# The last expert's down projection by column halves, each half scaled and scattered on its own

## The chip, the cores and the metric

The kernel runs on one core of one Trainium2 chip. The metric is device microseconds (us) of one execution, the median of several runs. Times inside a run are given from the start of the profiled span.

## The reference

One layer of a diffusion backbone: a token mixer (a bidirectional linear recurrence and an attention branch), then an expert-choice mixture of 16 experts over 1024 tokens of 1024 channels. The change lies in the mixture, cut here to its core:

```
aff = softmax(h @ w_router)                      # 1024 tokens x 16 experts
gate, idx = top_k(aff.T, 128)                    # each expert takes 128 tokens
xg  = h[idx]                                     # 128 x 1024 per expert
hid = silu(xg @ w_e_gate[e]) * (xg @ w_e_up[e])  # 128 x 1024
y   = (hid @ w_e_down[e]) * gate                 # 128 x 1024, scaled row by row
out = x + mod5 * zeros.at[idx].add(y)            # rows scattered, added to the output
```

## The kernel before

Weights and activations are fp32. Each matrix product is made of three matmuls (`mm3`, lines 98 to 100): both operands are split into a high part (`eh`, written by ScalarE as a cast, line 94) and a low rest (`el`, written by VectorE as a difference, line 95), and high x high, high x low and low x high are summed in PSUM. An expert's weight matrix comes as four loads of 1 MB (`load_raw`, line 990, issued by SyncE (SP), raw tiles `me` and `ma` in a ring of fifteen), each with two blocks of 128 rows and all 1024 columns. A split pair (`eh`, `el`) serves twelve matmuls. There are three buffers for `eh` and two for `el`, so the `el` of a pair can be written only when TensorE (PE) has read the `el` of two pairs before.

For each expert e, `up(e)`, `gate(e + 1)` and `down(e)` follow each other on PE, whose order is that of the code. `split_hid` turns the hidden 128 x 1024 tile by eight transposes (`hdt`) and splits it (`hdh` by ScalarE, `hdl` by VectorE (DVE)). `down(e)` runs 48 matmuls of 512 columns into a PSUM tile `w_e_down` of 128 x 1024, block of rows after block of rows, both column halves of each. Then DVE scales the whole tile once (`y`, line 1311, by the gate column `gcol` and the row `bc5`), and GpSimd (POOL) issues an indirect DMA (line 1312) that adds the 128 rows of `y`, 4 KB each, to the rows of the output named by `icol`. For all experts but the last, `split_hid(e)` is run in the middle of `gate(e + 1)`; for the last it stands ahead of `down`, with nothing between.

All scatters add into the same output, and each waits on POOL until the one before it has landed. The names DMASW and DMAHW below are the counters of landed DMAs that POOL and SP issued, and DVE_49, PE_49 and Activation_49 count the instructions that those engines have finished; an instruction that waits for a count waits for all earlier instructions of that engine too. DVE takes its instructions strictly in the order shown.

Of the kernel before, what the change touches and what calls it, by code (L numbers as in the profile page):

```python
# [19 lines left out]
F32 = mybir.dt.float32  # L20
F32R = mybir.dt.float32r
I32 = mybir.dt.int32
U32 = mybir.dt.uint32
AF = mybir.ActivationFunctionType
OP = mybir.AluOpType
AX = mybir.AxisListType

P = 128
D = 1024
KD = D // P  # L30
# [18 lines left out]
NE = 16  # L49
# [11 lines left out]
def layer_kernel(ctx: ExitStack, tc: tile.TileContext, I, rope_tab, out, dbg=None):  # L61
    nc = tc.nc
# [6 lines left out]
    x, w_in, w_ada = I["x"][0], I["w_in"][0], I["w_ada"][0]  # L69
# [17 lines left out]
    def pa(name="pa"):  # L87
        return ps["p"].tile([P, 1024], F32, name=name, tag="a", bufs=3)
# [4 lines left out]
    def split(h, l, src):  # L93
        nc.scalar.copy(h, src)  # L94
        nc.vector.tensor_tensor(l, src, h.bitcast(F32), OP.subtract)  # L95

    def mm3(o, lh, ll, rh, rl, start, stop):
        nc.tensor.matmul(o, lh, rh, start=start, stop=False)  # L98
        nc.tensor.matmul(o, lh, rl, start=False, stop=False)  # L99
        nc.tensor.matmul(o, ll, rh, start=False, stop=stop)  # L100
# [10 lines left out]
    def krows(w, c0, n):  # L111
        return w[:, c0:c0 + n].rearrange("(k p) n -> p k n", p=P)
# [142 lines left out]
    for m in range(2):  # L255
        for k in range(KD):
            if m == 0 or k < 4:
                nc.tensor.transpose(modv[:, m * KD + k, :], mrow[m][:, k * P:(k + 1) * P], ident[0:2, 0:2])
            else:
                for w in range(2):  # L260
# [5 lines left out]
                                   op0=OP.add, op1=OP.mult)  # L266
# [33 lines left out]
    n = n_early  # L300
# [30 lines left out]
    def nextw(shape, look=None):  # L331
        n = taken[0]
        assert items[n][1] == shape, (items[n], shape)
        taken[0] = n + (LOOK if look is None else look)
        fetch()
        taken[0] = n + 1
        return ahead[n]
# [31 lines left out]
    for j in range(NFIRST):  # L369
        h, l = nextw([KD, P])  # L370
# [48 lines left out]
    with pool("p2") as p2:  # L419
        wqh = p2.tile([P, KD, Z2], F32R, name="wqh")  # L420
        wql = p2.tile([P, KD, Z2], F32R, name="wql")
        for j in range(4):
            raw = wst.tile([P, 2, Z2], F32, name="wr", tag="wr", bufs=4)
# [3 lines left out]
        for j in range(2):  # L427
            raw = wst.tile([P, HEADS * QD], F32, name="wr", tag="wr", bufs=4)
# [3 lines left out]
        raw = wst.tile([P, 2, 512], F32, name="wr", tag="wr", bufs=4)  # L432
# [164 lines left out]
    if True:  # L597
# [106 lines left out]
        with tc.manual_schedule(engines={mybir.EngineType.Activation, mybir.EngineType.PE}):  # L704
# [4 lines left out]
            nlam, mag, z, s, s2, p_, p8, m8 = (sp[:, j] for j in range(8))  # L709
# [49 lines left out]
    for e in range(2):  # L759
        for nm, val in (("h", 1.0), ("l", 0.0)):  # L760
# [4 lines left out]
                                    op0=OP.mult, op1=OP.add)  # L765
# [92 lines left out]
    for b in range(KD):  # L858
        if b < 2:
            po, h, l = early[b]  # L860
            ro_mm(po, h, l, [KD - 1])
        else:
            h, l = nextw([KD, P])
            po = pa("ro")
# [30 lines left out]
    with pool("p5a") as p5a:  # L895
# [44 lines left out]
        with tc.manual_schedule(engines={mybir.EngineType.PE}):  # L940
            nxt = scores(0, 0)
            for i, (h, kt) in enumerate(steps):
                ph, pl = nxt
                if kt == 0:
                    po = [ps["p"].tile([P, 512], F32, name="po", bufs=2) for _ in range(2)]
# [13 lines left out]
                for n in range(2):  # L959
                    side(2 + n)  # L960
                    sl = slice(n * 512, (n + 1) * 512)
# [20 lines left out]
    xring, xsplit, raws, used = [], [], [], [0]  # L982

    def load_raw():

        n = len(raws)
        nm, e, k = worder[2 * n]
        pl, tg, nb = xring[n % (NME + NMA) >= NME]
        raw = pl.tile([P, 2, D], F32, name=tg, tag=tg, bufs=nb)
        nc.sync.dma_start(raw, krows(I[nm][0, e, k * P:(k + 2) * P, :], 0, D))  # L990
        raws.append(raw)

    pairs = []

    def split_raw():
        n = len(pairs)
        while len(raws) <= n:
            load_raw()
        h = xsplit[0].tile([P, 2, D], F32R, name="eh", bufs=3)
        l = xsplit[0].tile([P, 2, D], F32R, name="el", bufs=2)  # L1000
        split(h, l, raws[n])
        pairs.append((h, l))
# [6 lines left out]
    with pool("p6b", side="right") as p6b, pool("p6", side="right") as p6:  # L1009
# [119 lines left out]
        with tc.manual_schedule(engines={mybir.EngineType.PE}):  # L1129
            for hf in range(2):  # L1130
# [15 lines left out]
                else:  # L1146
# [17 lines left out]
                    while len(raws) < NME - 2:  # L1164
                        load_raw()
                for ph in (2 * hf, 2 * hf + 1):
                    if ph == 2:
                        for j in range(4):
                            wo[2, j] = wo[1, j]
                    for t in range(4):  # L1170
                        if t == 3 and ph in (0, 2):
                            load_wo(ph + 1, 0)
                        if t == 0 and ph in (1, 3):
                            for j in range(1, 4):
                                load_wo(ph, j)
                            if ph == 3:
                                while len(raws) < NME:
                                    load_raw()
                        if ph == 3 and t in (1, 2):
                            split_raw()  # L1180
                        xo(ph, t)
# [9 lines left out]
    gcol = consts.tile([P, NE], F32, name="gcol")  # L1191
    icol = consts.tile([P, NE], I32, name="icol")
    with pool("p7a", side="right") as p7a, pool("p7", side="right") as p7:
        xring.append((p7a, "ma", NMA))
        bc5 = p7.tile([P, D], F32, name="bc5")
        nc.sync.dma_start(bc5, bcast(mod_d[3], D))
        VT = ("hdh", "hdl", "y", "silu")
        def pq(name):
            return ps["p"].tile([P, 1024], F32, name=name, tag="q", bufs=4)
# [51 lines left out]
        XR, XG, G, H, HT = {}, {}, {}, {}, {}  # L1251
        out_rows = out[0]
# [9 lines left out]
        def tsplit(src, nm):  # L1262
            nb = 2 if nm == "xg" else 1
            hh = p7.tile([P, KD, P], F32R, name=nm + "h", tag=nm + "h", bufs=nb)
            ll = p7.tile([P, KD, P], F32R, name=nm + "l", tag=nm + "l", bufs=nb)
            tp = pq(nm + "t")
            for k in range(KD):
                nc.tensor.transpose(tp[:, k * P:(k + 1) * P], src[:, k * P:(k + 1) * P], ident)
            split(hh, ll, tp.rearrange("p (k t) -> p k t", t=P))
            return hh, ll  # L1270
# [6 lines left out]
        def proj(nm, e, op_, mid=None, km=4):  # L1277
            po = pq(nm)
            for k in range(KD):
                if k == km and mid:  # L1280
                    mid()
                h, l = wk(nm, e, k)
                for n in range(2):
                    sl = slice(n * 512, (n + 1) * 512)
                    mm3(po[:, sl], op_[0][:, k], op_[1][:, k], h[:, sl], l[:, sl], k == 0, k == KD - 1)
            return po
# [4 lines left out]
        def split_hid(e):  # L1291
            HT[e] = tsplit(H.pop(e), "hd")
# [7 lines left out]
        def up(e):  # L1300
# [2 lines left out]
            nc.vector.tensor_tensor(hid, po, hid, OP.mult)  # L1303
            H[e] = hid

        def down(e):
            if e + 1 == NE:
                split_hid(e)
            po = proj("w_e_down", e, HT.pop(e))
            y = p7.tile([P, D], F32, name="y", tag="y", bufs=1)  # L1310
            nc.vector.scalar_tensor_tensor(y, po, gcol[:, e:e + 1], bc5, op0=OP.mult, op1=OP.mult)  # L1311
            nc.gpsimd.indirect_dma_start(out=out_rows, out_offset=bass.IndirectOffsetOnAxis(ap=icol[:, e:e + 1], axis=0),  # L1312
                                         in_=y, in_offset=None, compute_op=OP.add)
# [7 lines left out]
        for e in range(NE):  # L1321
            up(e)
            if e + 2 < NE:
                gather(e + 2)
            if e + 1 < NE:
                gate(e + 1)
            down(e)
# [40 lines left out]
```

## Time and profile before

| | |
|---|---|
| median of 3 runs | 1769.93 us (1767.58 to 1776.2) |
| profiled execution, its own time | 1771.81 us |
| its span, first to last instruction | 1769.8 us |
| PE busy | 1687.1 us, 95% of the span |
| DVE busy | 1313.4 us, 74% |
| ACT (ScalarE) busy | 1014.9 us, 57% |
| POOL busy | 264.5 us, 15% |
| mean granted clock of TensorE | 0.981 of full speed |

PE is busy nearly all the time, but the busy share is a mean over the span. The change touches only what follows the last expert's hidden tile, some 22 us, and what counts there is which engine waits for which. The profiled execution is 1.88 us longer than the median.

### The profile page before, as it was taken

Reading aid. Unit: us, or ns where it says so; the run is one execution under the profiler, and the core shown is the slowest. Engines: PE = TensorE matmul, PEld = TensorE weight load, DVE = VectorE, ACT = ScalarE, POOL = GpSimd, SP = SyncE. Lnnn points to the kernel's source line nnn. Section 1 sums busy time; section 2 is a strip of 40 time slices with the busy share of each in tenths; the row PEclk is TensorE's granted clock in tenths of the full one; section 3 lists DMA queues with packets and bytes.
Section 4 is the critical chain, followed back from the end, with each engine's and each line's share of the span. In section 5 each row is a group of like instructions: output and inputs, shape, how many; then the busy total and the mean of one; then the engine's idle time right before and its main releaser. Section 6 shows DMA issues by size and latency. Waiting matters only on the chain.

```text
span 1769.8 us, 20838 instructions
## 1 busy us (share of the span) xinstructions
PE 1687.1 (95%) x7823; PEld 1356.9 (77%) x7823; DVE 1313.4 (74%) x1607; ACT 1014.9 (57%) x1105; POOL 264.5 (15%) x196
## 2 busy tenths in 40 slices
PE   8999999999999999999999999939999999999996
PEld 3788887888887877777777678827888888888885
DVE  4755456788886454787877657587999999989996
ACT  2533324876788313667776532316777777777773
POOL 1123331211221100111210100020121111112101
PEclk9999999999999999999999999969999999999999
DMA  8264444435443934000000355667999999999981
GB/s 328 100 181 101 108 121 140 131 126 167 155 144 117 318 136 152 28 28 28 29 1 1 138 199 213 234 261 286 379 395 391 403 399 381 399 402 380 389 309 24
DMA packets 174179, 363.72 MB, mean 206 GB/s; under 512 B 40160, under 2 KB 90744, under 8 KB 174080
## 3 DMA queue, kind: packets, MB, share of 16 engines
q1 hardware_dynamic: 168896, 343.54, 53.6%
q0 software_dynamic: 5184, 18.88, 4.0%
q8 instruction: 61, 1.00, 0.2%
q14 instruction: 38, 0.31, 0.0%
HBM read 314.84 MB, written 47.54 MB: 205 GB/s over the span
## 4 chain that ended last, share of the span: by engine, by line
PE 71%; DVE 11%; ACT 6%; issue 4%; DMA 4%; POOL 3%; SPq 0%; POOLq 0%; DVEq 0%; ACTq 0%
PE w_e_gate L99 3%; PE w_e_gate L100 3%; PE w_e_gate L98 3%; PE w_e_down L99 3%; PE w_e_down L100 3%; PE w_e_down L98 3%; PE w_e_up L99 3%; PE w_e_up L98 3%; PE w_e_up L100 3%; PE z L99 2%; PE z L98 2%; PE z L100 2%; PE pm L816 2%; POOL st L143 2%; PE s L98 2%
## 5 line engine op out<-in xcount | busy, mean ns | idle before, releaser
L95 DVE TENSOR_TENSOR el<-ma,eh 128x2048 fp32r<-128x2048 f32 x114 | 258.2, 2286 | 22.2 <-PE w_e_down L99 10.8
L94 ACT CAST eh<-ma 128x2048 fp32r<-128x2048 f32 x114 | 217.9, 1917 | 73.7 <-PE w_e_up L100 28.7
L95 DVE TENSOR_TENSOR el<-me,eh 128x2048 fp32r<-128x2048 f32 x78 | 176.9, 2287 | 16.6 <-ACT eh L94 6.0
L94 ACT CAST eh<-me 128x2048 fp32r<-128x2048 f32 x78 | 149.0, 1916 | 47.4 <-PE w_e_gate L100 17.3
L906 ACT ACTIVATE pr<-s 128x512 f32<-128x512 f32 x160 | 95.8, 599 | 77.2 <-PE s L100 75.8
L818 DVE TENSOR_REDUCE mx<-pm 128x1 f32<-128x320 f32 x256 | 114.4, 483 | 22.8 <-PE pm L816 20.6
L99 PE MATMUL z<-xl,wh 128*128 128x512 f32 x320 | 125.2, 392 | 1.9 <-DVE xl L280 1.9
L98 PE MATMUL z<-xh,wh 128*128 128x512 f32 x320 | 125.2, 393 | 1.0 <-DVE xh L279 0.8
L100 PE MATMUL z<-xh,wl 128*128 128x512 f32 x320 | 125.0, 391 | 1.2 <-POOL wl L326 1.2
L1312 POOL DMA_INDIRECT out_dram<-y,icol x16 | 52.3, 3268 | 469.9 <-DVE y L1311 469.9
L94 ACT CAST wh<-wr 128x1024 fp32r<-128x1024 f32 (+1 forms) x53 | 52.0, 980 | 116.1 <-PE z L99 55.0
L95 DVE TENSOR_TENSOR pl<-pr,ph 128x1024 fp32r<-128x1024 f32 x64 | 81.0, 1265 | 31.4 <-ACT ph L94 24.7
L99 PE MATMUL w_e_up<-el,xgh 128*128 128x512 f32 x256 | 100.7, 394 | 0.6 <-DVE el L95 0.6
L98 PE MATMUL w_e_gate<-eh,xgh 128*128 128x512 f32 x256 | 101.1, 395 | 0.2 <-ACT xgh L94 0.2
L99 PE MATMUL w_e_gate<-el,xgh 128*128 128x512 f32 x256 | 101.2, 395 | 0.0
L100 PE MATMUL w_e_gate<-eh,xgl 128*128 128x512 f32 x256 | 100.1, 391 | 0.8 <-DVE xgl L95 0.8
L98 PE MATMUL w_e_down<-eh,hdh 128*128 128x512 f32 x256 | 99.7, 389 | 1.1 <-ACT hdh L94 1.1
L98 PE MATMUL w_e_up<-eh,xgh 128*128 128x512 f32 x256 | 100.7, 393 | 0.0
L99 PE MATMUL w_e_down<-el,hdh 128*128 128x512 f32 x256 | 100.6, 393 | 0.0
L100 PE MATMUL w_e_down<-eh,hdl 128*128 128x512 f32 x256 | 99.9, 390 | 0.5 <-DVE hdl L95 0.5
L100 PE MATMUL w_e_up<-eh,xgl 128*128 128x512 f32 x256 | 99.8, 390 | 0.0
L816 PE MATMUL pm<-kh,qh 97*128 97x320 f32 x256 | 86.6, 353 | 7.0 <-DVE kl L95 4.1
(349 smaller groups left out, 4368.7 us busy)
## 6 DMA issues: line engine op xcount, KB each, us to landing
ma<-in_w_e_down_dram SPq DMA_DIRECT2D x40, 1024.0 KB, 9.4
ma<-in_w_e_up_dram SPq DMA_DIRECT2D x38, 1024.0 KB, 8.0
ma<-in_w_e_gate_dram SPq DMA_DIRECT2D x36, 1024.0 KB, 7.2
me<-in_w_e_gate_dram SPq DMA_DIRECT2D x28, 1024.0 KB, 7.0
me<-in_w_e_up_dram SPq DMA_DIRECT2D x26, 1024.0 KB, 8.2
me<-in_w_e_down_dram SPq DMA_DIRECT2D x24, 1024.0 KB, 9.8
wr<-in_w_in_dram SPq DMA_DIRECT2D x32, 512.0 KB, 4.5
wr<-in_w_ada_dram SPq DMA_DIRECT2D x32, 512.0 KB, 4.2
```

What stands on the lines that cost most here:

```text
L94: nc.scalar.copy(h, src)
L95: nc.vector.tensor_tensor(l, src, h.bitcast(F32), OP.subtract)
L98: nc.tensor.matmul(o, lh, rh, start=start, stop=False)
L99: nc.tensor.matmul(o, lh, rl, start=False, stop=False)
L100: nc.tensor.matmul(o, ll, rh, start=False, stop=stop)
L143: nc.gpsimd.tensor_tensor(ap, ap, h, OP.pow)
L816: nc.tensor.matmul(pm[:, 0:320], qh[:, t * P:(t + 1) * P], kh[:, g * 320:(g + 1) * 320], start=True, stop=True)
L818: nc.vector.tensor_reduce(mx[:, g, t:t + 1], pm[:, 0:320], axis=AX.X, op=OP.max)
L906: nc.scalar.activation(pr[:, sl], sp_, AF.Exp)
L1312: nc.gpsimd.indirect_dma_start(out=out_rows, out_offset=bass.IndirectOffsetOnAxis(ap=icol[:, e:e + 1], axis=0), in_=y, in_offset=None, com ...
```

## The change

The four loads of the last expert's `w_e_down` are cut differently: each now holds four blocks of 128 rows and 512 columns, in the order rows 0 to 511 and rows 512 to 1023 of the left columns, then the same of the right columns. `last_down` runs all 24 matmuls of the left half, then scales that half (128 x 512) and scatters it as rows of 512 columns into the output seen as 2048 rows of 512; then the same for the right half. The row numbers are 2 x `icol` and 2 x `icol` + 1, made by two DVE instructions of 128 x 1 (`ic2`). The first half's `y` has the buffer of `y`, the second's that of `silu`. Both halves of the product lie in one PSUM tile, as before.

```diff
+        if (nm, e) == ("w_e_down", NE - 1):
+
+            raw4, n4 = raw.rearrange("p a (b n) -> p (a b) n", b=2), k // 2
+            nc.sync.dma_start(raw4, krows(I[nm][0, e, n4 % 2 * 512:(n4 % 2 + 1) * 512, :], n4 // 2 * 512, 512))
+        else:
+            nc.sync.dma_start(raw, krows(I[nm][0, e, k * P:(k + 2) * P, :], 0, D))
...
+        def last_down(e):
+
+            split_hid(e)
+            hh, hl = HT.pop(e)
+            halves = out_rows.rearrange("s (a n) -> (s a) n", a=2)
+            ic2 = p7.tile([P, 2], I32, name="ic2")
+            for n in range(2):
+                nc.vector.tensor_scalar(ic2[:, n:n + 1], icol[:, e:e + 1], 2.0, float(n), op0=OP.mult, op1=OP.add)
+            po = pq("w_e_down")
+            for n in range(2):
+                sl = slice(n * 512, (n + 1) * 512)
+                for k in range(KD):
+                    m = used[0] // 2
+                    while len(pairs) <= m + k // 4:
+                        split_raw()
+                    h, l = (x.rearrange("p a (b n) -> p (a b) n", b=2)[:, k % 4] for x in pairs[m + k // 4])
+                    mm3(po[:, sl], hh[:, k], hl[:, k], h, l, k == 0, k == KD - 1)
+                used[0] += 4
+                y = p7.tile([P, 512], F32, name="y", tag=("y", "silu")[n], bufs=1)
+                nc.vector.scalar_tensor_tensor(y, po[:, sl], gcol[:, e:e + 1], bc5[:, sl], op0=OP.mult, op1=OP.mult)
+                nc.gpsimd.indirect_dma_start(out=halves, out_offset=bass.IndirectOffsetOnAxis(ap=ic2[:, n:n + 1], axis=0),
+                                             in_=y, in_offset=None, compute_op=OP.add)
+
         def down(e):
             if e + 1 == NE:
-                split_hid(e)
+                return last_down(e)
```

Three places show what moves. First PE, in the last `down`: the 23rd to the 26th of its 48 matmuls, and the 37th and 38th, which are the first of the fourth pair. Before:

```order
7158 L99 MATMUL w_e_down<-el,hdh 128x512
7159 L100 MATMUL w_e_down<-eh,hdl 128x512
7160 L98 MATMUL w_e_down<-eh,hdh 128x512
7161 L99 MATMUL w_e_down<-el,hdh 128x512 [waits DVE_49]
...
7172 L98 MATMUL w_e_down<-eh,hdh 128x512 [waits Activation_49]
7173 L99 MATMUL w_e_down<-el,hdh 128x512 [waits DVE_49]
```

Now, the same places:

```order
7158 L99 MATMUL w_e_down<-el,hdh 128x512
7159 L100 MATMUL w_e_down<-eh,hdl 128x512
7160 L98 MATMUL w_e_down<-eh,hdh 128x512 [waits DVE_49]
7161 L99 MATMUL w_e_down<-el,hdh 128x512
...
7172 L98 MATMUL w_e_down<-eh,hdh 128x512 [waits Activation_49]
7173 L99 MATMUL w_e_down<-el,hdh 128x512
```

The wait for DVE has moved from the 26th matmul, the first that reads the third pair's `el`, to the 25th, the first of the right half; and the 38th, the first that reads the fourth pair's `el`, no longer waits for DVE.

Second DVE, at the end of the program: the `el` of the last two pairs and what follows. Before:

```order
1361 L95 TENSOR_TENSOR hdl<-hdt,hdh 128x1024 [waits Activation_49]
1362 L95 TENSOR_TENSOR el<-ma,eh 128x2048 [waits DMAHW2_49,DVE_49,PE_49]
1363 L95 TENSOR_TENSOR el<-ma,eh 128x2048 [waits DVE_49,DMAHW3_49,PE_49,Activation_49]
1364 L1311 SCALAR_TENSOR_TENSOR y<-w_e_down,gcol,bc_9508 128x1024 [waits DMASW2_49,PE_49]
1365 L1364 UNCONDITIONAL_BRANCH
```

Now, the same instructions of DVE:

```order
1363 L95 TENSOR_TENSOR hdl<-hdt,hdh 128x1024 [waits Activation_49]
1364 L95 TENSOR_TENSOR el<-ma,eh 128x2048 [waits DMAHW2_49,DVE_49,PE_49]
1365 L95 TENSOR_TENSOR el<-ma,eh 128x2048 [waits DVE_49,DMAHW3_49,PE_49,Activation_49]
1366 L1330 SCALAR_TENSOR_TENSOR y<-w_e_down,gcol,bc_9508 128x512 [waits DMASW2_49,PE_49]
1367 L1330 SCALAR_TENSOR_TENSOR y<-w_e_down,gcol,bc_9508 128x512 [waits PE_49]
1368 L1392 UNCONDITIONAL_BRANCH
```

The first half's `y` stands behind the `el` of the fourth pair, which belongs to the right half.

Third POOL, its last DMAs (the scatters of the 14th and the 15th expert, and what the 16th has). Before:

```order
164 L1312 DMA out_dram<-y,icol 1024x1024 [waits DMASW7_49,DVE_49]
165 L1312 DMA out_dram<-y,icol 1024x1024 [waits DMASW1_49,DVE_49]
166 L1312 DMA out_dram<-y,icol 1024x1024 [waits DMASW2_49,DVE_49]
167 L1364 UNCONDITIONAL_BRANCH
168 L1364 ISA [waits barrier_Pool_Activation_PE_DVE_SP_gather]
```

Now, the same DMAs of POOL:

```order
164 L1340 DMA out_dram<-y,icol 1024x1024 [waits DMASW7_49,DVE_49]
165 L1340 DMA out_dram<-y,icol 1024x1024 [waits DMASW1_49,DVE_49]
166 L1331 DMA out_dram<-y,ic_13600 2048x512 [waits DMASW2_49,DVE_49]
167 L1331 DMA out_dram<-y,ic_13600 2048x512 [waits DMASW3_49,DVE_49]
168 L1392 UNCONDITIONAL_BRANCH
```

There is one scatter more, and it waits for the landing of the first half's scatter (DMASW3).

## Rows read from the trace of the kernel before

**Rows 1.** Timeline of DVE, the last stretch: start, us, instruction [idle before <- releaser].

```profile
1747.77 1.23 DVE L95 TENSOR_TENSOR hdl<-hdt,hdh 128x1024 fp32r<-128x1024 f32 x1
...
1754.21 2.29 DVE L95 TENSOR_TENSOR el<-ma,eh 128x2048 fp32r<-128x2048 f32 x1 [0.49 <-PE w_e_down L99]
1759.82 1.28 DVE L1311 SCALAR_TENSOR_TENSOR y<-w_e_down,gcol,bc 128x1024 f32<-128x1024 f32 x1 [3.32 <-PE w_e_down L100]
```

**Rows 2.** Timeline of PE in the last down projection.

```profile
1749.05 0.50 PE L100 MATMUL w_e_down<-eh,hdl 128*128 128x512 f32 x1 [0.53 <-DVE hdl L95]
1749.38 0.39 PE L98 MATMUL w_e_down<-eh,hdh 128*128 128x512 f32 x1
...
1753.95 0.39 PE L100 MATMUL w_e_down<-eh,hdl 128*128 128x512 f32 x1
1754.18 0.39 PE L98 MATMUL w_e_down<-eh,hdh 128*128 128x512 f32 x1
...
1759.39 0.39 PE L100 MATMUL w_e_down<-eh,hdl 128*128 128x512 f32 x1
```

**Rows 3.** Timeline of POOL, the last two scatters.

```profile
1734.07 3.37 POOL L1312 DMA_INDIRECT out_dram<-y,icol  x1 [31.50 <-DVE y L1311]
1761.38 1.55 POOL L1312 DMA_INDIRECT out_dram<-y,icol  x1 [23.95 <-DVE y L1311]
```

**Rows 4.** DMA issues, the last 15 us: queue, count, us from issue to landing.

```profile
out_dram<-y,icol POOLq DMA_INDIRECT x1, 6.1
```

**Rows 5.** Stretches after it: busy by engine, granted clock, DMA share, GB/s.

```profile
1763.50:1764.00 0.50, 0.00 (x0) 0.00 (x0) 0.00 (x0) 0.00 (x0) 0.00 (x0) 0.82 1.75 139
1766.50:1767.00 0.50, 0.00 (x0) 0.00 (x0) 0.00 (x0) 0.00 (x0) 0.00 (x0) 0.50 0.45 82
```

**Rows 6.** DVE instructions of 512 columns, grouped: count | busy, mean ns | idle before.

```profile
L1040 DVE TENSOR_TENSOR s<-mo,s 128x512 f32<-128x512 f32 x16 | 10.8, 683 | 1.7 <-PE mo L100 1.5
L214 DVE SCALAR_TENSOR_TENSOR macs<-wa,sc,macs 128x512 f32<-128x512 f32 x14 | 9.9, 748 | 8.4 <-DMA wa<-in_w_ada_dram 8.4
```

**Rows 7.** Waits of PE over the whole span: total, times, longest.

```profile
PE gz L98 <- ACT r L654: 4.5, 5, 2.0
...
PE qkt L803 <- DVE kl L95: 3.4, 1, 3.4
PE mo L98 <- DVE s L1040: 3.1, 1, 3.1
...
PE kv L100 <- DVE zl L95: 1.7, 1, 1.7
```

**Rows 8.** Stretches that hold these waits; clock third from the end.

```profile
225.00:240.00 15.00, 13.27 (x75) 11.50 (x74) 9.79 (x30) 4.38 (x10) 6.08 (x6) 1.00 0.51 116
300.00:315.00 15.00, 13.37 (x56) 11.15 (x57) 9.15 (x8) 10.04 (x13) 5.99 (x2) 0.89 0.40 124
615.00:630.00 15.00, 11.59 (x54) 9.43 (x53) 6.25 (x9) 3.57 (x6) 0.00 (x0) 0.89 0.84 290
990.00:1005.00 15.00, 11.91 (x43) 9.32 (x42) 13.88 (x24) 6.29 (x14) 4.79 (x8) 0.81 0.30 107
```

**Rows 9.** Timeline of PE behind the third of those waits.

```profile
1001.60 0.63 PE L98 MATMUL mo<-ath,wh 128*128 128x512 f32 x1
1002.03 0.63 PE L99 MATMUL mo<-atl,wh 128*128 128x512 f32 x1
```

**Rows 10.** Timeline of SP's queue, the last loads (the last expert's `w_e_down`).

```profile
1701.13 8.15 SPq L990 DMA_DIRECT2D ma<-in_w_e_down_dram  x4
```

**Rows 11.** The loads of w_e_down, issue to landing.

```profile
DMA to landing us min/median/max: 7.1/9.6/18.0
```

**Rows 12.** Timeline of ACT: the first cast of the last expert's w_e_down.

```profile
1738.87 1.92 ACT L94 CAST eh<-ma 128x2048 fp32r<-128x2048 f32 x1 [1.74 <-PE w_e_up L100]
```

**Rows 13.** Timeline of DVE behind the routing: first expert's tokens.

```profile
1199.70 1.23 DVE L95 TENSOR_TENSOR xgl<-xgt,xgh 128x1024 fp32r<-128x1024 f32 x1 [7.95 <-ACT xgh L94]
```

**Rows 14.** All sixteen scatters, issue to landing.

```profile
DMA to landing us min/median/max: 6.1/11.6/13.1
```

More of the change, by code (lines that the diff above doesn't have):

```diff
@@ L989, in load_raw @@
         raw = pl.tile([P, 2, D], F32, name=tg, tag=tg, bufs=nb)
-        nc.sync.dma_start(raw, krows(I[nm][0, e, k * P:(k + 2) * P, :], 0, D))
+        if (nm, e) == ("w_e_down", NE - 1):
[3 more added lines that the diff above has]
+            nc.sync.dma_start(raw, krows(I[nm][0, e, k * P:(k + 2) * P, :], 0, D))
         raws.append(raw)
```

## The prediction

> **What bounds the kernel here.** The page's table of busy shares says little: PE is busy 95% of the span, but the change lies in the last 22 us, where engines wait for one another. I read the timelines of the three engines that hand on to each other there, then the DMA views of the last scatter, then the whole run's waits of PE for something like what the new order does.
>
> The end is a line of single steps. PE's last matmul starts at 1759.39 [rows 2]; DVE scales the tile from 1759.82 to 1761.10 [rows 1]; POOL issues the scatter 0.28 us later, at 1761.38, for 1.55 us [rows 3]; it lands 6.1 us after that start, at 1767.5 [rows 4], its data moving from about 1763.5 to 1766.7 [rows 5]. The span ends at 1769.8, so 2.3 us of closing follow the landing. Of the last scatter's 6.1 us some 3.2 are data, and 2.9 (1.55 on POOL, about 0.6 before the data, about 0.75 behind them) do not depend on bytes. Whatever shifts PE's last matmul shifts the end; whatever shortens `y` or the last scatter takes from it in full.
>
> The reader is to see one more thing in DVE's rows. The fourth pair's `el` starts at 1754.21 and ends at 1756.50 [rows 1], because its buffer comes free only when PE has read the second pair's, near the 24th of the 48 matmuls (1753.95, [rows 2]). PE needs that `el` only at the 38th matmul. So before, DVE is late without anyone waiting.
>
> **The change part by part.** *PE's new wait.* Still 48 matmuls, so no work is added. But the 25th now waits for DVE, and the 38th no longer does, so the count that the 25th waits for covers the fourth pair's `el`; in the built program it is that of the first half's `y`. Both halves are in one PSUM tile, and the matmuls of the right half are made to wait until DVE has read the left. That `y` stands on DVE behind the fourth `el`. So: `el` ends 1756.50; `y` of 512 columns takes 0.75, from the same operation on 512 columns (0.748), with 0.68 as the lower bound from an operation that reads PSUM [rows 6]; it ends 1757.25. PE goes on 0.05 later, as it did from `hdl` (1747.77 + 1.23 = 1749.00, then 1749.05, [rows 1, 2]): 1757.30 instead of 1754.18, 3.1 us late. The first matmul behind a wait is followed after 0.33 us instead of 0.23 [rows 2]: 0.1 more. **+3.2**. The queue behind that matmul is the right half, its `y`, its scatter, hence the end. Nothing covers it.
>
> *The clock.* PE stands still for some 2.9 us, from the end of the 24th at 1754.34 (1753.95 + 0.39). Waits of that size occurred before: 2.0, 3.4 and 3.1 us [rows 7]. In each of the 15 us stretches that hold them the mean clock is below 1: 0.89, 0.89, 0.81 [rows 8]. At 1.2 instead of 2.4 GHz that is 3.3, 3.3 and 5.7 us (0.11 x 15 / 0.5, and so on). The third is the nearest row there is: there too PE waited for a DVE operation of 512 columns, and behind it matmuls followed each other every 0.43 us instead of 0.23 [rows 9]. The wait of 1.7 us left the clock of its stretch at 1.00 [rows 7, 8]. Price: 3.3 us at the low level hold 8 matmuls that would take 1.7 us, so **+1.6**; bounds 0 (no fall) and +4.8 (all 24 at 0.43). I take +1.6, which two of three show.
>
> *The last `y`.* 0.75 instead of 1.28: **-0.5**.
>
> *The last scatter.* 128 rows of 2 KB instead of 4 KB. No row shows an accumulating scatter of such rows. Bounds: the 3.2 us of data stay (they go by rows) or halve (by bytes), 0 to -1.6. I take the middle, **-0.8**; the landing is then 5.3 us after the issue. The Trainium skill (DMA: Bandwidth & Descriptors, section "Anatomy of one DMA — SWDGE (gpsimd) path") speaks against such a cut: each DMA issued by GpSimd costs about 2 us however small, plus its bytes at 436 GB/s. By that page, as an estimate, half the bytes save 0.6 and not 0.8, and the sum below would be 0.2 higher; the trace has 6.1 us for 512 KB where the page's formula gives 3.2, so here the measurement decides.
>
> *The first scatter, and the wait of the second for it.* Issued at 1757.25 + 0.28 = 1757.53, it lands by 1763.6 even at the full 6.1. The right half's `y` ends at 1759.82 + 3.2 + 0.75 = 1763.8 at the full clock (1765.4 with the fall), POOL could issue at 1764.05 or later, so the wait is covered by 0.4 us or more: 0. If POOL needed 3.37 as beside the `el` of the scatter before [rows 3], the landing would be 1765.4 and 1.4 would show at the full clock, none with the fall.
>
> *At nothing.* The loads in half rows are issued from 1701.1 to 1709.3 [rows 10] and landed 7 to 18 us after issue [rows 11]; the first cast that reads them starts at 1738.87 [rows 12], so they may take 10 us longer. The casts and differences have the same 128 x 2048. The two `ic2` instructions stand where DVE was idle for 7.95 us [rows 13]; without that cover they would cost at most 1.23 each, what 1024 columns take there.
>
> Sum: 3.2 + 1.6 - 0.5 - 0.8 = **+3.5**. The profiled execution would go from 1771.81 to 1775.3; against the median, 1769.93, it gives **1773.4**.
>
> **The rivals.** *The clock holds.* For it: the wait of 1.7 us left it at 1.00. Against: all three waits of 2.0 us or more. +1.9, 1771.8.
>
> *PE isn't held* (the 25th matmul waits for something done earlier). Then `y` ends at 1760.6, but the second scatter stands behind the first's landing, 1762.8 to 1763.6, instead of 1761.38: +1.4 to +2.2, less 0.8 to 0 for the data: about +1.4, 1771.3. Only if the first scatter landed within 4.5 us (2.9 fixed, halved data), at 1762.0, and the second saved 1.6, would it gain: -1.0, 1768.9. Against it: PE's order rows, where the 38th matmul needs no wait any more.
>
> *The two scatters in series decide, and it is slower.* Place: the second one's wait on POOL. With a landing time L for each the end is 1757.53 + 2L + 2.3. It passes the point of half a percent (8.85 us, about what a measurement of this kernel can tell from no change) at L = 9.4. The median of the sixteen is 11.6 [rows 14], which would give 1783.0, +13.2, 1783.1. Against it: that median is with 1 MB loads on the same DMA engines; the last scatter, with none, took 6.1, and there are none here.
>
> **How the numbers follow.** Wait and fallen clock, 0.62: 1773.4, its own range 1771 to 1777. Wait, clock holds, 0.22: 1771.8. PE not held, 0.08, a gain in a third of it. Series of slow scatters, 0.05. The rest, 0.03, is what no row shows. The range reaches from the best end of the third case, 1769, to a right half all at the low clock with no data saved (3.2 + 4.8 - 0.5 = 7.5): 1777.4. By the same cases: faster by over 0.5% 0.02, slower 0.06 (the fourth case and a little of the rest), within 0.92. So the work saved at the end is real and smaller than the wait that takes its place.
>
> **What would show it.** PE idle for some 2.9 us between the 24th and 25th matmul of the last `down`, released by DVE's `y`; granted clock 0.5 for some 3 us behind it and matmuls 0.43 us apart; `y` twice, near 0.75; two scatters of 256 KB, the second one's data in 1.6 to 3.2 us, and POOL waiting for `y`, not for the landing. I'd be wrong if PE runs through, if a scatter of half rows takes 9 us, or if all of the experts' matmuls change pace: `ic2` moves its pool's other tiles by a few bytes, and a pitch other than 0.23 there would show it.

## The result and the profile after

| | before | after |
|---|---|---|
| median, six runs each | 1770.28 us (1765.62 to 1776.2) | 1782.87 us (1781.67 to 1784.58) |
| ratio, 95% interval | | 1.0074 (1.0058 to 1.0090) |
| profiled execution, its span | 1771.81, 1769.8 us | 1781.67, 1779.4 us |

The changed kernel is 12.6 us slower, outside the range. I read its profile from the end backwards, as before. First PE: the first expert's transposes, then the last `down`.

```profile
1193.82 1.09 PE L1273 MATMUL xgt<-ident,xg 128*128 128x128 f32 x8 [0.83 <-DMA xg<-h_d,icol]
...
1754.65 0.50 PE L98 MATMUL w_e_down<-eh,hdh 128*128 128x512 f32 x1 [1.10 <-ACT hdh L94]
...
1760.91 0.40 PE L100 MATMUL w_e_down<-eh,hdl 128*128 128x512 f32 x1
1764.17 0.79 PE L98 MATMUL w_e_down<-eh,hdh 128*128 128x512 f32 x1 [2.87 <-DVE y L1330]
1764.77 0.63 PE L99 MATMUL w_e_down<-el,hdh 128*128 128x512 f32 x1
1765.19 0.63 PE L100 MATMUL w_e_down<-eh,hdl 128*128 128x512 f32 x1
...
1771.12 0.40 PE L100 MATMUL w_e_down<-eh,hdl 128*128 128x512 f32 x1
```

The wait is there, 2.87 us ahead of the 25th matmul, released by the first half's `y`. Behind it matmuls follow each other every 0.43 us. The stretches of the end, with the clock third from the end, show for how long:

```profile
1754.60:1761.40 6.80, 6.13 (x24) 4.34 (x24) 3.75 (x3) 1.91 (x1) 0.00 (x0) 1.00 0.00 0
1761.40:1764.20 2.80, 0.03 (x1) 0.03 (x1) 2.72 (x2) 0.00 (x0) 0.00 (x0) 0.97 0.00 0
1764.20:1767.70 3.50, 3.50 (x9) 2.78 (x10) 0.00 (x0) 0.00 (x0) 1.55 (x1) 0.53 0.37 40
1767.70:1771.60 3.90, 3.82 (x17) 2.74 (x15) 0.04 (x1) 0.00 (x0) 0.00 (x0) 1.00 0.18 32
```

DVE and POOL of the same stretch, and from the DMA view the two scatters with their median time from issue to landing:

```profile
1761.17 2.29 DVE L95 TENSOR_TENSOR el<-ma,eh 128x2048 fp32r<-128x2048 f32 x1 [0.56 <-PE w_e_down L99]
1763.38 0.74 DVE L1330 SCALAR_TENSOR_TENSOR y<-w_e_down,gcol,bc 128x512 f32<-128x512 f32 x1
1764.40 1.55 POOL L1331 DMA_INDIRECT out_dram<-y,ic  x1 [20.29 <-DVE y L1330]
1771.56 0.75 DVE L1330 SCALAR_TENSOR_TENSOR y<-w_e_down,gcol,bc 128x512 f32<-128x512 f32 x1 [7.44 <-PE w_e_down L100]
1772.59 1.55 POOL L1331 DMA_INDIRECT out_dram<-y,ic  x1 [6.64 <-DVE y L1330]
```

```profile
out_dram<-y,ic POOLq DMA_INDIRECT x2, 4.5
```

`y` stands behind the fourth `el` and takes 0.74; the second scatter waits for its `y` and not for the first one's landing; they land 4.5 us after their issue where the undivided one took 6.1 [rows 4]. From the last `down`'s first matmul to the end of the span that makes 24.75 us (1779.4 - 1754.65). Before, it was 22.01, by this row of the trace of before, which stands with the one of the first expert's transposes:

```profile
1197.45 1.09 PE L1268 MATMUL xgt<-ident,xg 128*128 128x128 f32 x8 [0.77 <-DMA xg<-h_d,icol]
...
1747.79 0.50 PE L98 MATMUL w_e_down<-eh,hdh 128*128 128x512 f32 x1 [1.10 <-ACT hdh L94]
```

So the part that the prediction worked on has grown by 2.7 us. The rest lies ahead of it. From the transposes to that matmul, called the **expert stage** below, it is 550.34 us before (1747.79 - 1197.45) and 560.83 after: **+10.5 us**, in a stage whose instructions and order the change leaves alone. (2.7 + 10.5 is 13.2; the spans differ by 9.6 because the stages ahead of the experts were 3.6 us shorter in that execution. Where they end differs from run to run, 1193.8 to 1203.1 us in the thirteen profiles of kernels in which these stages have the same code and places; the expert stage repeats to 0.2 us.) A stretch of 510 us inside the stage, before and then after:

```profile
1225.00:1735.00 510.00, 509.83 (x2350) 419.16 (x2349) 463.45 (x236) 376.82 (x221) 65.00 (x28) 1.00 0.98 376
```

```profile
1225.00:1735.00 510.00, 509.93 (x2308) 412.50 (x2307) 457.64 (x231) 370.16 (x218) 64.11 (x27) 1.00 0.99 374
```

PE is busy without a break at full clock in both, and gets 42 instructions fewer through. So it isn't a wait and not the clock: each matmul takes longer. The groups of matmuls of that stretch (count | busy, mean ns), before and then after:

```profile
L98 PE MATMUL w_e_gate<-eh,xgh 128*128 128x512 f32 x238 | 94.0, 395 | 0.0
L98 PE MATMUL w_e_up<-eh,xgh 128*128 128x512 f32 x228 | 89.7, 394 | 0.0
L98 PE MATMUL w_e_down<-eh,hdh 128*128 128x512 f32 x240 | 93.4, 389 | 0.0
```

```profile
L98 PE MATMUL w_e_gate<-eh,xgh 128*128 128x512 f32 x233 | 93.2, 400 | 0.0
L98 PE MATMUL w_e_up<-eh,xgh 128*128 128x512 f32 x224 | 89.3, 399 | 0.0
L98 PE MATMUL w_e_down<-eh,hdh 128*128 128x512 f32 x235 | 92.8, 395 | 0.0
```

The rows shown are those of line 98: five to six ns more on each. Those of line 100 gain five, those of line 99 two to four, and the weight loads ahead of them keep their mean of 187 to 188 ns. The only thing of the change that reaches that far back is a place in memory: in the built program (places don't stand in a trace) `ic2` has 32 bytes at the top of pool `p7`, and all other tiles of the pool (`xgh`, `xgl`, `hdh`, `hdl`, `bc5`, `y`, `silu`, `xg`) stand 32 bytes lower than before, when they stood at multiples of 512. The theory of the experiments is this **shift**. The rival is that something else in the change slows the stage: the half-row loads, the two `ic2` instructions.

### The profile page after: what moved, and what is told of

It reads as the page before. It is cut to its first block, busy times and chain, and to the rows that moved or that the text cites. A ratio compares the mean times of both kernels' runs of the same rounds, so it can differ in the third digit from the quotient of the medians.

```text
span 1779.4 us, 20844 instructions
## 1 busy us (share of the span) xinstructions
PE 1697.3 (95%) x7823; PEld 1357.4 (76%) x7823; DVE 1321.0 (74%) x1610; ACT 1015.3 (57%) x1105; POOL 265.8 (15%) x197
## 4 chain that ended last, share of the span: by engine, by line
PE 71%; DVE 12%; ACT 6%; issue 4%; DMA 4%; POOL 3%; POOLq 0%; SPq 0%; DVEq 0%; ACTq 0%
PE w_e_gate L100 3%; PE w_e_gate L99 3%; PE w_e_gate L98 3%; PE w_e_up L99 3%; PE w_e_up L98 3%; PE w_e_up L100 3%; PE w_e_down L100 3%; PE w_e_down L98 3%; PE w_e_down L99 3%; PE pm L816 2%; PE z L99 2%; POOL st L143 2%; PE z L98 2%; PE z L100 2%; PE s L98 2%
## 5 line engine op out<-in xcount | busy, mean ns | idle before, releaser
L95 DVE TENSOR_TENSOR el<-ma,eh 128x2048 fp32r<-128x2048 f32 x114 | 259.8, 2289 | 26.0 <-PE w_e_down L99 12.6
```

## The experiments

Totals are against runs of the kernel before on the same chip (median 1774.73 us for the first four, 1774.63 for the next four); the kernel before takes some 4 us more there than in the runs of the result, so ratios are compared. The last five have one execution each, and of them only the expert stage is read.

**1. The change without the shift.** `ic2` takes the tile of `sl4`, which is dead by then.

```diff
-            sl4 = p7.tile([P, 4, 32], F32, name="sl4")
+            sl4 = p7.tile([P, 4, 32], F32, name="sl4", tag="sl4", bufs=1)
...
-            ic2 = p7.tile([P, 2], I32, name="ic2")
+            ic2 = p7.tile([P, 2], I32, name="ic2", tag="sl4", bufs=1)
```

> The changed kernel, with ic2 put into the tile of sl4 (dead by then), so that every tile of pool p7 stands at its address of before. The changed kernel takes 12.6 us more than before, and its expert stage up to the last down's first matmul 10.5 us more. Shift theory (the 32 bytes by which ic2 moves the pool's other tiles slow all of the experts' matmuls): the expert stage is back at its 550 us and the matmuls' pitch at 0.227 us, and what is left is the last down's own part, +2 to +4 us, so 1772 to 1775. Rival (the stage is longer because of the half-row loads of the last matrix, the extra instructions or another part of the change): 1781 to 1784, as the changed kernel.

Measured: ratio 1.0017 (1.0005 to 1.0028), +3.0 us; expert stage 550.52 us. The 510 us stretch holds as many instructions as before the change:

```profile
1225.00:1735.00 510.00, 509.82 (x2350) 418.92 (x2349) 464.05 (x235) 377.14 (x221) 64.08 (x27) 1.00 0.99 379
```

The rival falls: half-row loads, the `ic2` instructions and the rest of the change leave the stage as it was, to 0.2 us. What is left, +3.0, is the last `down`'s own.

**2. The shift without the change.** The kernel before, with an unused tile in the place of `ic2`.

```diff
+            if e + 1 == NE:
+                nc.gpsimd.memset(p7.tile([P, 8], F32, name="pad"), 0.0)
             y = p7.tile([P, D], F32, name="y", tag="y", bufs=1)
```

> The kernel before, with nothing of the change but an unused tile of 32 bytes, made last in pool p7, so that its other tiles stand 32 bytes lower, as in the changed kernel. Shift theory: the expert stage grows by 10.5 us, so 1779 to 1782, with w_e matmuls at 0.395 to 0.400 us mean. Rival (other parts of the change): 1769 to 1772, as before.

Measured: 1.0055 (1.0038 to 1.0073), +9.8 us; expert stage 560.85, that of the changed kernel to 0.02. The shift alone does it. And it does it where nothing else is at work: behind the last `el` only PE is busy. The stretches from the first to the last matmul start there, of the kernel before and of this one:

```profile
1756.67:1759.39 2.72, 2.72 (x13) 2.25 (x12) 0.00 (x0) 0.00 (x0) 0.00 (x0) 1.00 0.00 0
```

```profile
1771.29:1774.32 3.03, 3.03 (x15) 2.43 (x13) 0.00 (x0) 0.00 (x0) 0.00 (x0) 1.00 0.00 0
```

DVE, ACT, POOL and the DMA engines stand at 0 in both, and the starts lie 0.2267 us apart before (2.72 by 12) and 0.2331 here (3.03 by 13). So it isn't another engine or a transfer that gets in TensorE's way.

**3. Half of the shift.** The same unused tile, made just ahead of `gather(0)`.

```diff
+        nc.gpsimd.memset(p7.tile([P, 8], F32, name="pad"), 0.0)
         with tc.manual_schedule(engines={mybir.EngineType.PE}):
             gather(0)
```

> The kernel before with the same unused tile made ahead of the xg tiles: bc5, hdh, hdl, y and silu stand 32 bytes lower, xg, xgh and xgl where they were. If the price is in the stationary operands that TensorE loads, only the down matmuls (hdh, hdl: a third of all) pay: about a third of 10.5, so 1773 to 1774.5, with gate and up at their pitch of before and w_e_down slower. If it is in the tiles that DVE, ACT or the DMA touch (bc5, y, silu), all three projections are paced as in the changed kernel, 1779 to 1782. If the shift is nothing: 1769 to 1772.

Measured: 1.0013 (1.0000 to 1.0026), +2.3 us; expert stage 554.54, +4.2, somewhat more than the third of 10.5 that was expected. The groups:

```profile
L98 PE MATMUL w_e_gate<-eh,xgh 128*128 128x512 f32 x240 | 94.7, 395 | 0.0
L98 PE MATMUL w_e_up<-eh,xgh 128*128 128x512 f32 x224 | 88.1, 393 | 0.0
L98 PE MATMUL w_e_down<-eh,hdh 128*128 128x512 f32 x236 | 93.2, 395 | 0.0
```

Only `w_e_down` has its duration of the changed kernel; gate and up have that of before, though `bc5`, `y` and `silu` have moved. So the price is TensorE's own, paid by the matmuls whose stationary operand has moved. The stage has 720 of them (the last `down` is not in it); by the groups they take 5 to 6 ns more, which makes some 3.8 of the 4.2 us.

**4, 5 and 9 to 11. Other sizes.** The edit of the second experiment, with 16, 128, 24, 32 and 64 in place of 8 elements.

> The kernel before with an unused tile of 64 bytes made last in pool p7: all other tiles of the pool 64 bytes lower. If 64 bytes is the size of what is fetched (tiles at a multiple of 64 are as good as at a multiple of 512): 1769 to 1772, as before. If any odd place within 512 bytes costs: 1778 to 1782. If the shift is nothing: 1769 to 1772 here and in the run with 32 bytes alike.

> The kernel before with an unused tile of 512 bytes made last in pool p7: every tile of the pool moves, and each keeps its place within a multiple of 512 bytes. The expert stage (from the first expert's xg transposes to the last down's first matmul) took 550.3 us before, 560.8 with all tiles 32 bytes lower, 553.1 with 64. If what costs is the place of the stationary operands within a small multiple of bytes: 550.3 +- 0.5, and the total as before, +-1. If it is any move (the distance to other tiles, another region): 553 or more, total +2 or more.

> The kernel before with an unused tile of 96 bytes made last in pool p7; what is read is the expert stage (first expert's xg transposes to the last down's first matmul) in the profile. So far: 550.3 to 550.5 us with the tiles at a multiple of 512 bytes, 560.85 with them 32 lower, 553.1 with them 64 lower. If an odd multiple of 32 is what costs most (a fetch of 64 bytes that each piece then straddles): 560 to 561, as with 32. If the price falls off with the distance: below 553.

> The same with 128 bytes. If a multiple of 128 is enough: 550.3 to 550.6. If the remaining 2.7 us at 64 come from any place off a multiple of 512: 552.5 to 553.5.

> The same with 256 bytes. If a multiple of 128 or 256 is enough: 550.3 to 550.6. If only multiples of 512 are free of it: 552.5 to 553.5.

| tiles of p7 lower by, bytes | 0 | 32 | 64 | 96 | 128 | 256 | 512 |
|---|---|---|---|---|---|---|---|
| expert stage, us | 550.34 | 560.85 | 553.05 | 561.33 | 559.30 | 550.44 | 550.46 |

Ratios were taken for 64 and 512: 1.0010 (1.0001 to 1.0019) and 1.0001 (0.9991 to 1.0011). So it isn't any move that costs: 256 and 512 bytes are free. The guesses on the kind of step fail, though: 64 isn't as good as 0, and 128 is far worse than 64. If the tile's own place counted, a multiple of 128 should do no worse than one of 64; this raised the question of the next two.

**12 and 13. Place, or distance.** TensorE reads two operands: the stationary ones (`xgh`, `xgl`, `hdh`, `hdl`) had moved, the moving ones (`eh`, `el`) never. A pad of 32 bytes at the foot of the other side of the memory is left out, which puts `eh` and `el` 32 bytes lower; in the second of the two the unused tile of experiment 2 puts the stationary ones 32 lower as well.

```diff
-    ctx.enter_context(tc.tile_pool(name="padl", bufs=1)).tile([P, PADL], F32, name="padl")
+    pass
```

> The kernel before without the 32-byte pad at the foot of the left side: every tile of that side, eh and el among them (the moving operands of all the experts' matmuls), stands 32 bytes lower, the stationary operands (xgh, xgl, hdh, hdl) at their multiples of 512. Read from the expert stage in the profile, 550.3 us before; other stages have tiles on that side too, so the total isn't read. If only the place of the stationary operand within 256 bytes counts: 550.3 to 550.6. If it is the distance between the two operands, or any operand's place: 555 to 562.

> As the run before, and the unused tile of 32 bytes in pool p7 as well: stationary and moving operands both 32 bytes lower, so the distance between them is that of the kernel before. If the distance decides: 550.3 to 550.6. If the stationary operand's own place decides: 560.5 to 561.5. If each operand's place costs for itself: more than the larger of the two single shifts.

Measured: expert stage 560.77 us with the moving operands alone lower, 550.40 with both. The groups, moving operands alone and then both:

```profile
L98 PE MATMUL w_e_gate<-eh,xgh 128*128 128x512 f32 x236 | 94.4, 400 | 0.0
L98 PE MATMUL w_e_down<-eh,hdh 128*128 128x512 f32 x224 | 88.6, 395 | 0.0
```

```profile
L98 PE MATMUL w_e_gate<-eh,xgh 128*128 128x512 f32 x240 | 94.8, 395 | 0.0
L98 PE MATMUL w_e_down<-eh,hdh 128*128 128x512 f32 x229 | 89.2, 389 | 0.0
```

So my reading up to here, that the stationary operand has to stand well, falls too: with both operands 32 bytes off their places of before, nothing is lost. The distance between the two decides, and as far as these distances show, changing it by a multiple of 256 bytes is free.

The pad left out here (`padl`, 32 bytes, line 72) stands in the kernel before for no use of its own, and so does `padr` (480 bytes, line 73); without the first, the expert stage takes 10.4 us more. It serves an earlier stage as well. The matmuls `z`, with operands of other pools (min/median/max, ns), before and then with both of the experts' operands lower:

```profile
L99 PE MATMUL z<-xl,wh x320: 387/389/502, 40.3 to 504.8; 128*128 128x512 f32 x160
```

```profile
L99 PE MATMUL z<-xl,wh x320: 392/396/794, 37.5 to 512.3; 128*128 128x512 f32 x160
```

Their median is 389 before, after and in experiment 2, and 394 to 396 in both runs without the pad; which of their operands moved, no run here shows.

**6. PE not held.** Experiment 1, with a PSUM tile for each half.

```diff
-            po = pq("w_e_down")
-            for n in range(2):
+            with tc.manual_schedule(engines={mybir.EngineType.PE}):
+                for n in range(2):
+                    po = pq("w_e_down")
```

> The changed kernel without the shift (ic2 in the tile of sl4), and a PSUM tile for each half of the last down, so that the 25th matmul has nothing to wait for; TensorE's order in the last down is the program's. Without the two tiles this kernel took +3.0 us against before, with a wait of 2.88 us and 3.4 us at half clock behind it. If these two are the price, as the prediction has it (3.2 and 1.6): no gap ahead of the 25th matmul and clock 1.00 in the second half. What is left then: the last y 0.5 less, the last scatter's landing 1.6 less, but the first half's y still stands behind the fourth pair's el, so its scatter lands about 8.1 us behind the 24th matmul and the second scatter waits for it some 1.5 us: -0.6 against before, between -2 and +0.5. If the price is elsewhere (the half-row loads, ic2's own instructions, two scatters): still +2 to +3.

Measured: 1.0008 (0.9997 to 1.0019), +1.4 us; the clock is 1.00 over the whole last `down` and the 25th matmul follows the 24th after 0.23 us. POOL:

```profile
1757.71 1.55 POOL L1332 DMA_INDIRECT out_dram<-y,ic  x1 [20.00 <-DVE y L1331]
1763.33 1.55 POOL L1332 DMA_INDIRECT out_dram<-y,ic  x1 [4.07 <-DMA out_dram<-y,ic]
```

The held PE had been hiding a second wait. Now the second `y` ends at 1760.84, and its scatter stands until 1763.33 behind the first one's landing, 2.2 us and not the 1.5 expected: the first one landed 4.9 us after its issue, at 1762.6, and POOL went on 0.7 us later. In this profile the end part is 22.54 us, 0.5 more than before (2.2 for the wait, less 0.5 for `y` and 1.2 for the landing). The +1.4 lies outside the range that was expected, -2 to +0.5, but its interval reaches from -0.5 to +3.4.

**7. The first `y` early as well.** The `el` of the last two pairs and the `eh` of the last take free tiles of the ring `ma`, and DVE's order at the end is `hdl`, third `el`, fourth `el`, `y`, `y`.

```diff
+        if n == 12 * NE - 1:
+            h = xring[1][0].tile([P, 2, D], F32R, name="eh", tag="ma", bufs=NMA)
+        else:
+            h = xsplit[0].tile([P, 2, D], F32R, name="eh", bufs=3)
+        if n >= 12 * NE - 2:
+            l = xring[1][0].tile([P, 2, D], F32R, name="el", tag="ma", bufs=NMA)
+        else:
+            l = xsplit[0].tile([P, 2, D], F32R, name="el", bufs=2)
...
+            with tc.manual_schedule(engines={mybir.EngineType.PE, mybir.EngineType.DVE, mybir.EngineType.Activation}):
+                split_hid(e)
+                hh, hl = HT.pop(e)
+                split_raw()
+                split_raw()
+                for n in range(2):
+                    po = pq("w_e_down")
```

> As the kernel with two PSUM tiles, and the first half's y stands behind nothing: the third and fourth pair's el and the fourth pair's eh take free tiles of the ring ma, so that they are made before the 24th matmul; TensorE's, DVE's and ACT's order in the last down is the program's. The first half's scatter then lands about 6 us behind the 24th matmul, ahead of the second half's y at about 6.4, and nothing waits: -0.5 for the last y and -1.6 for the last landing, -2.1 against before (between -3 and -1). If DVE is late with el in the new order, or the scatters wait for each other all the same: -0.5 to +1.

Measured: 0.9988 (0.9978 to 0.9998), -2.1 us (-3.9 to -0.4): the one version here that is shown to beat both kernels, if only by what a measurement can just tell. Its POOL:

```profile
1755.69 1.55 POOL L1339 DMA_INDIRECT out_dram<-y,ic  x1 [17.94 <-DVE y L1338]
1761.16 1.55 POOL L1339 DMA_INDIRECT out_dram<-y,ic  x1 [3.92 <-DVE y L1338]
```

The second scatter is released by its own `y` again; the end part is 20.19 us, 1.8 less than before.

**8. One PSUM tile, `y` early.** Experiment 7 with `po = pq("w_e_down")` ahead of the loop.

> As the kernel before this one in the list, but with one PSUM tile for both halves again, as the change has it: the 25th matmul waits for the first half's y, which now starts right behind the 24th matmul. Wait: about 0.3 + 0.75 = 1.1 to 1.3 us in place of 2.88. If a gap of that length leaves the clock at 1.00, as the gaps up to 1.73 us of the kernel before did: 1.2 us over the kernel with two tiles, -0.9 against before. If the clock falls here too: +1.6 more, +0.7 against before.

Measured: 0.9997 (0.9986 to 1.0008), -0.5 us (-2.5 to +1.4): this can't tell the -0.9 of a clock that holds from the +0.7 of one that falls. The trace of the one profiled execution can:

```profile
1756.34 0.39 PE L100 MATMUL w_e_down<-eh,hdl 128*128 128x512 f32 x1
1757.66 0.47 PE L98 MATMUL w_e_down<-eh,hdh 128*128 128x512 f32 x1 [0.94 <-DVE y L1338]
```

Two stretches, one of the last `down`'s start and one behind that wait:

```profile
1748.00:1752.00 4.00, 3.96 (x9) 2.67 (x10) 3.43 (x3) 3.41 (x2) 0.00 (x0) 0.50 0.00 0
1757.70:1761.70 4.00, 4.00 (x18) 3.33 (x19) 0.00 (x0) 0.00 (x0) 1.55 (x1) 1.00 0.48 54
```

With the fourth `el` out of the way the wait is 0.94 us in place of 2.87, and the clock behind it stays at 1.00 (the second stretch; of the first, which this edit doesn't touch, the last section speaks). So most of the change's own wait was the `el` in front of `y`, as the prediction said, and in this execution the fall of the clock went with it.

## Why the prediction was wrong, point by point

**The step that failed** is "At nothing", where the two `ic2` instructions are costed and the tile that they write is not. The text knew of the move ("`ic2` moves its pool's other tiles by a few bytes") and put it under what would make it wrong, with no price and no chance of its own; and I read no row of the stage itself, since all instructions that changed are at the end. One row would have given the weight of the risk: TensorE is busy there without a break for 510 us, so nothing hides a slower matmul. The two pads in the kernel's text, whose purpose the prediction didn't ask, were a second sign. The move cost +10.5 us in place of 0: the changed kernel's 560.83 us, experiment 1's 550.52 without the shift and experiment 2's 560.85 with nothing else.

The other steps, by the profile after:

- *PE's wait, +3.2.* The 25th matmul starts 3.26 us after the 24th in place of 0.23: +3.0. Right, and from the cause named: experiment 6 takes the shared PSUM tile away, and no wait is left; experiment 8 takes only the `el` away, and 0.94 us are left.
- *The clock, +1.6.* From the 25th to the 48th matmul it takes 6.95 us (1771.12 - 1764.17) in place of 5.21 [rows 2]: +1.7, of which 0.1 is the slower pace of the whole stage. Right; the rival that the clock holds was wrong for a wait of 2.87 us and is what experiment 8 shows for 0.94.
- *The last `y`, -0.5.* 0.75 in place of 1.28: right.
- *The last scatter, -0.8.* It landed in 4.5 us: -1.6. Mis-sized, by having taken the middle: the saving is the whole of the bound for data that go by bytes. In the profiles of experiments 1 and 6 to 8 the half scatters land after 4.7 to 4.9 us, so some of the 1.6 is spread between executions. The formula of the Trainium skill (DMA: Bandwidth & Descriptors, "Anatomy of one DMA — SWDGE (gpsimd) path"), by which I had estimated a saving of 0.6, is off by more; the measurement decides.
- *The second scatter's wait, 0.* Right for this kernel: POOL went on with `y`. And where PE isn't held, it showed, as the rival had it. That rival's +1.4 and the +1.4 measured (experiment 6, -0.5 to +3.4) agree in part by luck: that profile's end part grew by 0.5, because its last scatter landed 1.2 us sooner than the undivided one, where the rival had at most 0.8.
- *The loads in half rows, 0.* Right by experiment 1.

With the slower pace of the first 24 matmuls (1754.65 to 1760.91, 6.26 us in place of 6.16) these make 3.0 + 1.7 - 0.5 - 1.6 + 0.1 = 2.7, which is what the end part grew by; +3.5 was forecast, and the change without the shift measured +3.0 (0.9 to 5.0). So the account of the end was right in its mechanism, with the scatter's saving too small, and it was a fifth of the whole: 2.7 + 10.5 = 13.2, against 12.6 between the medians.

## What to carry to other kernels

A new tile in a pool can be an edit to every matmul that has an operand in that pool: compare the places of the tiles before and after, reckon with up to 2% of the stage if TensorE's two operands move against each other (10.5 of 550 us here), and keep the distance between them what it was, or change it by a multiple of 256 bytes, by giving the new tile a dead one's place or by padding. Pads already in a kernel are a hint that places matter there. If a stage in which nothing was changed gets longer with its engine busy throughout, look at mean durations by group before looking for waits. And when a wait goes, look at what it hid: here PE's wait hid the scatters' wait for each other, and only the version without either was faster than before by more than the noise.

## What the runs showed of the hardware that was not expected

- TensorE's pace depends on the distance between the two operands it reads. The Trainium skill (TensorE: Matmul & The Clock Gate, "Step-by-step: what each phase is for") says that there are two independent read ports, and that loading the next weights takes no read bandwidth from the running matmul. It names no dependence on places, and the runs here show one: 550.3 to 550.5 us for the expert stage with the distance unchanged or changed by 256 or 512 bytes, against 553 to 561 for the four other changes, with weight loads of the same duration. Whether loads and matmuls meet at the same part of the memory, or something else, no run here shows; nor was the dependence measured at other shapes and types, or at distances between those of the table.
- The clock can fall behind several small gaps, and does so in some executions only. At the start of the last `down` PE has gaps of 1.32 and 1.10 us in every profile, by `silu` and `hdh`, and then one of up to 0.53, by `hdl`. Behind them matmuls were 0.43 us apart for some 3 us in seven of the fifteen profiles, and not in the other eight, those of before and after among them. In experiment 8 the clock had fallen ahead of the third gap, and matmuls were that slow for some 6 us; the first stretch shown there is part of it, at a granted clock of 0.50 (1.2 of 2.4 GHz). In experiments 1 and 8 this cost 1.6 and 2.3 us (the first 24 matmuls took 7.76 and 8.48 us there, 6.16 before), as much as all that was gained here, so the last `down` of two single profiles can be compared only where their clocks agree.
